# Hybrid decoder step (mLSTM and gated DeltaNet): residual rows loaded by halves, two weight pieces in gate buffers, one ring of three buffers for head outputs

## The chip, the cores and the metric

The kernel runs on one core of a Trainium2 chip. Its time is device microseconds from launch to end. Before the change the median of three runs is 1212.48 us (1211.23 to 1213.59). A traced execution gives the profile; times in it count from the span's first instruction.

## The reference

One layer of a decoder, for a prompt of 1024 tokens (with 16 learned tokens in front) and for 8 sample tokens with stored states:

```python
u = _rms_norm(x, norm_w) @ w_in              # 1024 -> 8216 columns
# split into q, k, v, o, z and gates of 4 mLSTM heads, q, k, v, z and gates of 8 GDN heads
hm = chunked mLSTM(q_m, k_m, v_m, li, lf)    # matrix memory, per head 128 x 256
ym = head_rms(hm) * w_mnorm * sigmoid(o_m) * silu(z_m)
og = chunked gated delta rule(silu(conv(q_g, k_g, v_g)), beta, g)   # state per head 128 x 128
yg = head_rms(og) * w_gnorm * silu(z_g)
y  = concat([ym, yg]) @ w_out                # 2048 -> 1024
return x + y, states                         # and a final RMSNorm with final_norm_w
```

All of it is float32. The outputs are both groups' rows and all new states.

## The kernel before

Every matrix product on TensorE (PE) takes its operands split into a high and a low part in a faster float32 format and adds three of the four partial products. The projection keeps the normalised, transposed x in SBUF (tiles xht and xlt, high and low part) and runs over 64 weight tiles of 128 columns. Between its matmuls PE gets the work of the heads: the chunk chains (`gdn_chain`, L1029, then `mlstm_chain`, L1264), their inverses, the sample group, and the gates (`gate`, L1473), which load a head's outputs from DRAM (tile ht), scale them on ScalarE (ACT), transpose them on PE (hT) and multiply them by the gate values.

The order of all instructions is written out by a planner at build time (`Plan`, L65). Each piece of work is a generator that yields what it waits for. `Plan.run` (L224) keeps a modelled clock for each engine and each time takes the first thread that can go on; the projection, followed by the output products, is the filler that runs otherwise. `note` (L99) advances the clocks; `Plan.old` holds, for tiles that come from a `Ring` (L245), the modelled end of the last read of the buffer, before which a write does not start. Tiles made by `w` (L453), two buffers deep unless stated, have no such entry. Each engine executes its instructions in the written order, and nearly all DMAs are issued in order on SyncE (SP).

Head outputs go through such tiles. A GDN chunk writes `oo` (L1094, 128 columns, two buffers) on VectorE (DVE), squares it on ACT and stores it to h_d in DRAM. An mLSTM chunk copies its numerator and denominator from PSUM to `mho` (L1335, 258 columns, two buffers) on ACT and stores it in the same way. Each head has a chunk 0 without an output and eight chunks with one.

The output projection is a Strassen-like scheme of seven products over two halves of the tokens and two halves of the columns (`PRODUCTS`, L1618; `out_products`, L1737). A product has eight steps k of four token tiles t, each three matmuls of 512 columns, 96 in all. Its right operands are four items made from pieces of W_out (512 KB each, 16 pieces): GpSimd (POOL) adds or subtracts two pieces (`right_sums`, L1678), ACT rounds the sum to the high part and DVE takes the low part (`right_splits`, L1699; tiles owh and owl). Its left operands are gate results, reloaded from DRAM (s_d, c_d; 256 KB each, `left_loads`, L1715) for every product after the first, and split by ACT and DVE. `drain` (L1770) adds or subtracts a finished product to rows of x, half a row of 512 columns at a time, on DVE: product 0 into the second halves (h = 1) of both token halves, product 1 into a second half, product 2 into first halves (h = 0). A product takes the PSUM banks of the one two before it, so those must be drained first.

`weight_loads` (L1654) loads the pieces in a fixed order into places that `places` (L1634) hands out: two buffers of the sample work (ebuf), two of the projection's weights (wout0, wout1), and, once the projection has ended (event "x") and xht and xlt are free, twelve of the 16 places there. Region places 12 and 13 hold sums, 14 the first residual rows, 15 the sample rows. Pieces 0 to 7 serve product 0, where item i is made from pieces 2i and 2i + 1. `residual` (L1812) loads eight tiles xr of 128 rows by 1024 columns (512 KB each) as the steps k = 4 to 7 of product 0 are used: one into the region, two into buffers of the ring r_v, five into the ring r_gm, which gates use for ht, y and yg and whose last five wait until gate 7 is through.

The profile puts all instructions on line L56, that of the helper that records them, so its rows are told apart by tile names.

Of the kernel before, what the change touches and what calls it, by code (L numbers as in the profile page):

```python
# [20 lines left out]
P = 128  # L21
D = 1024
# [42 lines left out]
class Plan:  # L65
# [102 lines left out]
    def shares(self, op, out, ins):  # L168
# [2 lines left out]
            return False  # L171
        return sum(int(np.prod(x.shape[1:])) > 1 for x in ins) > 1 or op in ("tensor_copy", "tensor_scalar", "memset")

    def when(self, x, wait):
        t, e = self.done.get(self.key(x), (0.0, ""))
        return t + (self.DMA if e == "dma" else wait + self.POOL * (e == "pool"))
# [68 lines left out]
class Ring:  # L245
# [7 lines left out]

    def get(self, *args):
        i = self.idle.pop(0)
        t, read = self.make(i, *args), self.plan.read
        self.old, self.names[i] = self.names.get(i), t.tensor.name
        read[t.tensor.name] = self.plan.old[t.tensor.name] = read.get(self.old, 0.0) + self.plan.LAT
        return i, t

    def free(self, i):
# [31 lines left out]
def hymba_kernel(ctx: ExitStack, tc: tile.TileContext, a: dict, o: dict):  # L293
# [157 lines left out]
    hs = gp.tile([P, 16, NS], F32, name="hs")  # L451

    def w(tag, shape, name, bufs=2):  # L453
        return wk.tile([P] + shape, F32, tag=tag, name=name, bufs=bufs)

    def ring(tag, bufs):
        tags = [f"{tag}{i}" for i in range(bufs)] + ["B", "E"]
# [6 lines left out]
    def has(*key):  # L464
        return lambda: key in done
# [563 lines left out]
    def gdn_chain(h):  # L1029
# [32 lines left out]
        for c in range(NCH):  # L1062
# [26 lines left out]
            if c == 0:  # L1089
                dve.tensor_copy(Sn, up[:, 0:P])  # L1090
            else:
                dve.scalar_tensor_tensor(
                    out=Sn, in0=S, scalar=egend[:, c, h : h + 1], in1=up[:, 0:P], op0=ALU.mult, op1=ALU.add)
                oo = w("oo", [P], f"oo{h}_{c}")  # L1094
                dve.tensor_tensor(out=oo, in0=qs, in1=up[:, P : 2 * P], op=ALU.add)
                jq = w("jm", [256], f"jo{h}_{c}", bufs=1)[:, 0:P]
                act.activation(jq, oo, AF.Square, accum_out=ss[:, 1, c - 1 : c])
                sp.dma_start(h_d[8 + h, :, c - 1, :], oo)
# [165 lines left out]
    def mlstm_chain(h):  # L1264
# [50 lines left out]
        for c in range(NCH):  # L1315
# [16 lines left out]
            if c + 1 < NCH:  # L1332
                prepare(c + 1)
            if c > 0:
                ho = w("mho", [258], f"mho{h}_{c}")  # L1335
                act.copy(ho[:, 0:257], nm[:, 0:257])
                st = w("st", [4], f"mst{h}_{c}")
                jk = w("jm", [256], f"mjk{h}_{c}", bufs=1)
# [295 lines left out]
    def places():  # L1634
# [4 lines left out]
        for i in range(2):  # L1639
            yield has("split", i)  # L1640
            t = wp.tile([P, 2 * HALF], F32, tag="wr", name=f"wout{i}")
            plan.read[t.tensor.name] = plan.read.get(wrs[-2], 0.0)
            wrs.append(t.tensor.name)
            yield t
        yield has("x")
        for tag, old in (("xh", xht), ("xl", xlt)):
            t = xp.tile([P, 32 * 264], F32, tag=tag, name=f"region{tag}")
# [1 line left out]
            plan.war.add(t.tensor.name)  # L1649
            region.extend(t[:, D * i : D * i + D] for i in range(8))  # L1650
        done.add(("region",))
        yield from region[0:12]

    def weight_loads():  # L1654

# [114 lines left out]
    def drain(p, t, pt):  # L1770

        to = PRODUCTS[p][1]
        yield lambda: all((c, t) in xr for c, _, _ in to) and (p == 0 or ("drain", p - 1, t) in done)
        for c, h, op in to:
            x_ = xr[c, t][:, HALF * h : HALF * h + HALF]
            yield x_
# [35 lines left out]
    def residual():  # L1812

        yield has("region")
        for n, (c, t) in enumerate([(c, t) for t in range(4) for c in range(2)]):
            if c == 0:
                yield has("used", 0, 4 + t)
            if n == 0:
                x_ = region[14]
            else:  # L1820
                r = r_v if n < 3 else r_gm
                yield lambda: len(pairs) == DEEP and r.can() and (n < 3 or ("y", 7) in done)
                _, x_ = r.get([D], f"xr{c}_{t}")
            q0 = HALF * c + P * t
            sp.dma_start(x_, a["x_p"][q0 : q0 + P, :])
            xr[c, t] = x_
        xs_ = region[15][0:NS]
        sp.dma_start(xs_, a["x_s"])
        xr["s"] = xs_
        yield has("product", 3)  # L1830
        sp.dma_start(fwb, a["final_w"].partition_broadcast(P))
        done.add(("fw",))
# [204 lines left out]
```

## Time and profile before

| | |
|---|---|
| median of three runs | 1212.48 us |
| the profiled execution | 1213.45 us, its span 1211.7 us |
| PE busy | 1190.0 us (98%) |
| DVE busy | 851.3 us (70%) |
| ACT busy | 602.7 us (50%) |
| POOL busy | 487.4 us (40%) |
| DMA | 154.86 MB, mean 128 GB/s |
| mean granted TensorE clock | 0.995 of full |
| chain that ended last | PE 84%, DVE 5%, issue 4%, DMA 3%, ACT 2% |

A matmul's end is modelled, so a busy PE is not a PE at its peak. SPq is SP's queue of DMA issues: a long duration of a merged row of issues means that the later of them waited. PEclk is the granted clock as a share of 2.4 GHz, and a DMA share of 1 means that all 16 engines are busy.

### The profile page before, as it was taken

What the parts mean: (1) busy time and instruction counts of PE and PEld (TensorE: products, weight loads), DVE (VectorE), ACT (ScalarE), POOL (GpSimd) and SP (SyncE); (2) the same over time, 40 slices, a digit from 0 to 9 for tenths busy, and PEclk for the clock granted to TensorE, in tenths of its full rate; (3) what the DMA queues carried; (4) which work ended last, traced back from release to release, by engine and by line L of the source; (5) the groups of instructions that cost most, each with busy time, mean ns of one, the idle gap of its engine ahead of it and who ended that gap; (6) DMA issues with size and microseconds to landing.
All of it is one profiled execution on the core that took longest, in us unless ns stands there. A gap on an engine that the chain in (4) does not pass through costs nothing.

```text
span 1211.7 us, 23025 instructions
## 1 busy us (share of the span) xinstructions
PE 1190.0 (98%) x8314; PEld 1109.5 (92%) x8314; DVE 851.3 (70%) x2069; ACT 602.7 (50%) x1894; POOL 487.4 (40%) x648
## 2 busy tenths in 40 slices
PE   9999999999999999999999999998999999989997
PEld 7999999999999999999998899988999999866885
DVE  6789787587968688863266565636666764779886
ACT  7544355667465656554545344434544433333544
POOL 3105877828584847773021413410011111442332
PEclk9999999999999999999999999998999999999999
DMA  6032213221211221122132343445777876682342
GB/s 240 19 98 86 77 47 88 80 61 55 84 58 43 85 78 51 45 65 58 46 102 79 142 142 109 143 148 161 264 275 285 301 287 225 248 309 86 98 157 87
DMA packets 85932, 154.86 MB, mean 128 GB/s; under 512 B 26665, under 2 KB 48385, under 8 KB 85818
## 3 DMA queue, kind: packets, MB, share of 16 engines
q1 hardware_dynamic: 85624, 153.23, 37.6%
q8 instruction: 65, 1.06, 0.4%
q14 instruction: 49, 0.40, 0.1%
q10 hardware_dynamic: 194, 0.17, 0.0%
HBM read 107.65 MB, written 45.71 MB: 127 GB/s over the span
## 4 chain that ended last, share of the span: by engine, by line
PE 84%; DVE 5%; issue 4%; DMA 3%; ACT 2%; POOL 1%; SPq 0%; POOLq 0%; ACTq 0%; DVEq 0%
PE pjg L56 20%; PE pjm L56 13%; PE op L56 11%; PE pjz L56 7%; PE pjo L56 7%; PE pjzm L56 6%; PE up L56 4%; PE tp L56 3%; PE sk L56 2%; PE mnm L56 2%; PE hT L56 1%; PE mup L56 1%; PE kk L56 1%; PE E L56 1%; PE W L56 1%
## 5 line engine op out<-in xcount | busy, mean ns | idle before, releaser
L56 PE MATMUL pjg<-xht,whg 128*128 128x350 f32 (+6 forms) x624 | 197.7, 324 | 1.0 <-ACT xht L56 1.0
L56 PE MATMUL pjg<-xlt,whg 128*128 128x350 f32 (+6 forms) x624 | 197.1, 323 | 0.0
L56 PE MATMUL pjg<-xht,wlg 128*128 128x350 f32 (+6 forms) x592 | 191.1, 326 | 0.0
L56 POOL TENSOR_TENSOR tmp<-B,E 33x31 f32<-33x31 f32 (+15 forms) x248 | 148.5, 599 | 76.0 <-DMA B<-nd 57.2
L56 POOL TENSOR_TENSOR E<-E,tmp 33x31 f32<-33x31 f32 (+15 forms) x248 | 155.2, 626 | 19.4
L56 PE MATMUL op<-owh,left 128*128 128x512 f32 x448 | 143.1, 399 | 1.8 <-DVE left L56 1.7
L56 PE MATMUL pjm<-xht,wlm 128*128 128x350 f32 (+2 forms) x384 | 126.4, 329 | 0.0
L56 PE MATMUL pjm<-xht,whm 128*128 128x350 f32 (+2 forms) x384 | 126.4, 329 | 0.0
L56 PE MATMUL pjm<-xlt,whm 128*128 128x350 f32 (+2 forms) x384 | 126.1, 328 | 0.0
L56 PEld LDWEIGHTS pjg<-xht,whg 128*128 128x128 f32 x624 | 116.5, 189 | 1.8 <-issue 1.2
L56 PEld LDWEIGHTS pjg<-xlt,whg 128*128 128x128 f32 x624 | 116.5, 189 | 0.5
L56 PEld LDWEIGHTS pjg<-xht,wlg 128*128 128x128 f32 x592 | 110.9, 189 | 0.4
L56 PEld LDWEIGHTS op<-owh,left 128*128 128x128 f32 x448 | 84.6, 189 | 24.8 <-DVE left L56 3.2
L56 DVE SCALAR_TENSOR_TENSOR kq<-cr,prm,kq 128x346 f32<-128x346 f32 (+7 forms) x147 | 92.7, 634 | 11.4 <-ACT kq L56 7.8
L56 PE MATMUL op<-owl,left 128*128 128x512 f32 x224 | 89.0, 397 | 2.1 <-DVE owl L56 2.1
L56 PEld LDWEIGHTS pjm<-xht,wlm 128*128 128x128 f32 x384 | 72.5, 189 | 0.8 <-issue 0.4
L56 PEld LDWEIGHTS pjm<-xlt,whm 128*128 128x128 f32 x384 | 72.4, 188 | 0.6 <-issue 0.4
L56 PEld LDWEIGHTS pjm<-xht,whm 128*128 128x128 f32 x384 | 72.4, 188 | 0.2
L56 POOL TENSOR_TENSOR ebuf<-ebuf,wb 128x1024 f32<-128x1024 f32 x8 | 15.4, 1930 | 129.4 <-DMA ebuf<-mvb_d 129.4
L56 PE MATMUL pjzm<-xlt,whzm 128*128 128x344 f32 x192 | 62.8, 327 | 0.0
L56 PE MATMUL pjz<-xlt,whz 128*128 128x344 f32 x192 | 62.8, 327 | 0.0
L56 PE MATMUL pjzm<-xht,wlzm 128*128 128x344 f32 x192 | 62.5, 326 | 0.0
(353 smaller groups left out, 3185.1 us busy)
## 6 DMA issues: line engine op xcount, KB each, us to landing
wrg<-in_wt SPq DMA_DIRECT2D x23, 512.0 KB
left<-c_d SPq DMA_DIRECT2D x40, 256.0 KB
wrm<-in_wt SPq DMA_DIRECT2D x16, 512.0 KB
ht<-h_d SPq DMA_DIRECT2D x16, 512.0 KB
gm<-rows_d SPq DMA_DIRECT2D x8, 576.0 KB
xt<-in_x_p SPq DMA_DIRECT2D x8, 512.0 KB
wrz<-in_wt SPq DMA_DIRECT2D x8, 512.0 KB
h_d<-oo SPq DMA_DIRECT2D x64, 64.0 KB
```

The lines of the kernel that those rows point to most:

```text
L56: r = f(*args, **kw)
```

## The change

The three edits, and one that goes with the third:

- The eight tiles xr are filled by halves. The second halves (256 KB each) are loaded as steps k = 0 to 3 of product 1 are used, the first halves as the same steps of product 2 are used. A drain waits for its own halves. Three tiles lie in the region (places 10, 11 and 14), two in r_v, three in r_gm.
- Weight pieces 4 and 5 go to two buffers of r_gm, once gate 5 and all GDN gates are through and two buffers are free; they no longer wait for the end of the projection. The region holds ten pieces.
- `oo` and `mho` become one tag of three buffers of 258 columns.
- `w` reports every tile that it makes to the planner, which then knows the last read of its buffer, as it did for rings.

```diff
--- before.py
+++ after.py
@@ -171,6 +171,10 @@
             return False
         return sum(int(np.prod(x.shape[1:])) > 1 for x in ins) > 1 or op in ("tensor_copy", "tensor_scalar", "memset")

+    def follow(self, t, old):
+
+        self.read[t.tensor.name] = self.old[t.tensor.name] = self.read.get(old, 0.0) + self.LAT
+
     def when(self, x, wait):
         t, e = self.done.get(self.key(x), (0.0, ""))
         return t + (self.DMA if e == "dma" else wait + self.POOL * (e == "pool"))
@@ -253,9 +257,9 @@

     def get(self, *args):
         i = self.idle.pop(0)
-        t, read = self.make(i, *args), self.plan.read
+        t = self.make(i, *args)
         self.old, self.names[i] = self.names.get(i), t.tensor.name
-        read[t.tensor.name] = self.plan.old[t.tensor.name] = read.get(self.old, 0.0) + self.plan.LAT
+        self.plan.follow(t, self.old)
         return i, t

     def free(self, i):
@@ -451,7 +455,12 @@
     hs = gp.tile([P, 16, NS], F32, name="hs")

     def w(tag, shape, name, bufs=2):
-        return wk.tile([P] + shape, F32, tag=tag, name=name, bufs=bufs)
+        t, names = wk.tile([P] + shape, F32, tag=tag, name=name, bufs=bufs), wnames.setdefault(tag, [""] * bufs)
+        plan.follow(t, names[-bufs])
+        names.append(t.tensor.name)
+        return t
+
+    wnames = {}

     def ring(tag, bufs):
         tags = [f"{tag}{i}" for i in range(bufs)] + ["B", "E"]
@@ -1091,7 +1100,7 @@
             else:
                 dve.scalar_tensor_tensor(
                     out=Sn, in0=S, scalar=egend[:, c, h : h + 1], in1=up[:, 0:P], op0=ALU.mult, op1=ALU.add)
-                oo = w("oo", [P], f"oo{h}_{c}")
+                oo = w("oo", [258], f"oo{h}_{c}", 3)[:, 0:P]
                 dve.tensor_tensor(out=oo, in0=qs, in1=up[:, P : 2 * P], op=ALU.add)
                 jq = w("jm", [256], f"jo{h}_{c}", bufs=1)[:, 0:P]
                 act.activation(jq, oo, AF.Square, accum_out=ss[:, 1, c - 1 : c])
@@ -1332,7 +1341,7 @@
             if c + 1 < NCH:
                 prepare(c + 1)
             if c > 0:
-                ho = w("mho", [258], f"mho{h}_{c}")
+                ho = w("oo", [258], f"mho{h}_{c}", 3)
                 act.copy(ho[:, 0:257], nm[:, 0:257])
                 st = w("st", [4], f"mst{h}_{c}")
                 jk = w("jm", [256], f"mjk{h}_{c}", bufs=1)
@@ -1642,6 +1651,11 @@
             plan.read[t.tensor.name] = plan.read.get(wrs[-2], 0.0)
             wrs.append(t.tensor.name)
             yield t
+        yield lambda: all(("y", k) in done for k in (5, *range(8, 16))) and r_gm.can(2)
+        for i in range(2):
+            t = r_gm.get([D], f"wout{2 + i}")[1]
+            yield plan.read[t.tensor.name]
+            yield t
         yield has("x")
         for tag, old in (("xh", xht), ("xl", xlt)):
             t = xp.tile([P, 32 * 264], F32, tag=tag, name=f"region{tag}")
@@ -1649,7 +1663,7 @@
             plan.war.add(t.tensor.name)
             region.extend(t[:, D * i : D * i + D] for i in range(8))
         done.add(("region",))
-        yield from region[0:12]
+        yield from region[0:10]

     def weight_loads():

@@ -1770,7 +1784,7 @@
     def drain(p, t, pt):

         to = PRODUCTS[p][1]
-        yield lambda: all((c, t) in xr for c, _, _ in to) and (p == 0 or ("drain", p - 1, t) in done)
+        yield lambda: all(("xr", c, h, t) in done for c, h, _ in to) and (p == 0 or ("drain", p - 1, t) in done)
         for c, h, op in to:
             x_ = xr[c, t][:, HALF * h : HALF * h + HALF]
             yield x_
@@ -1812,18 +1826,23 @@
     def residual():

         yield has("region")
-        for n, (c, t) in enumerate([(c, t) for t in range(4) for c in range(2)]):
-            if c == 0:
-                yield has("used", 0, 4 + t)
-            if n == 0:
-                x_ = region[14]
-            else:
-                r = r_v if n < 3 else r_gm
-                yield lambda: len(pairs) == DEEP and r.can() and (n < 3 or ("y", 7) in done)
-                _, x_ = r.get([D], f"xr{c}_{t}")
-            q0 = HALF * c + P * t
-            sp.dma_start(x_, a["x_p"][q0 : q0 + P, :])
-            xr[c, t] = x_
+        for h in (1, 0):
+            for t in range(4):
+                yield has("used", 2 - h, t)
+                for c in range(2):
+                    if h:
+                        n = 2 * t + c
+                        if n < 3:
+                            x_ = region[(10, 11, 14)[n]]
+                        else:
+                            r = r_v if n < 5 else r_gm
+                            yield lambda: len(pairs) == DEEP and r.can() and (n < 5 or ("y", 7) in done)
+                            x_ = r.get([D], f"xr{c}_{t}")[1]
+                            plan.split(x_, HALF, r.old)
+                        xr[c, t] = x_
+                    q0, hs_ = HALF * c + P * t, slice(HALF * h, HALF * h + HALF)
+                    sp.dma_start(xr[c, t][:, hs_], a["x_p"][q0 : q0 + P, hs_])
+                    done.add(("xr", c, h, t))
         xs_ = region[15][0:NS]
         sp.dma_start(xs_, a["x_s"])
         xr["s"] = xs_
```

## Rows read from the trace of the kernel before

**Rows 1.** Stretches of 30 us: length, busy time of each engine (instructions), PEclk, DMA share, GB/s.

```profile
0.00:30.00 30.00, 26.99 (x171) 23.22 (x172) 19.27 (x37) 21.01 (x44) 10.71 (x26) 1.00 0.65 242
...
810.00:840.00 30.00, 26.23 (x171) 23.96 (x161) 15.33 (x58) 15.60 (x55) 1.90 (x1) 1.00 0.51 162
...
840.00:870.00 30.00, 29.51 (x177) 28.67 (x178) 24.56 (x72) 17.10 (x54) 0.00 (x0) 0.89 0.63 209
...
1050.00:1080.00 30.00, 29.11 (x124) 22.75 (x122) 23.85 (x32) 8.09 (x15) 9.50 (x5) 1.00 0.84 321
...
1080.00:1110.00 30.00, 26.98 (x141) 16.99 (x141) 29.76 (x33) 11.88 (x23) 11.81 (x5) 0.94 0.25 81
```

**Rows 2.** Timeline of PE: start, us, instruction, then idle before and its releaser.

```profile
840.49 2.52 PE L56 MATMUL hT<-ident,ht 128*128 128x128 f32 x8 [3.09 <-ACT ht L56]
...
1074.85 0.73 PE L56 MATMUL op<-owh,left 128*128 128x512 f32 x2 [0.87 <-DVE left L56]
...
1082.20 0.64 PE L56 MATMUL op<-owl,left 128*128 128x512 f32 x1 [2.15 <-DVE owl L56]
```

**Rows 3.** Timeline of ACT, 831 to 843 us.

```profile
831.41 0.39 ACT L56 COPY mho<-mnm 128x257 f32<-128x257 f32 x1
...
839.23 0.38 ACT L56 COPY mho<-mnm 128x257 f32<-128x257 f32 x1 [6.54 <-DMA h_d<-mho]
...
840.05 2.43 ACT L56 ACTIVATE ht<-ht,rsg 128x128 f32<-128x128 f32 x8
```

**Rows 4.** Timeline of SP's DMA issues, 825 to 840 us.

```profile
825.50 0.36 SPq L56 DMA_DIRECT2D h_d<-mho  x1
...
826.92 1.67 SPq L56 DMA_DIRECT2D ht<-h_d  x1
...
828.69 0.29 SPq L56 DMA_DIRECT2D vb_d<-vsb  x1
...
832.27 0.32 SPq L56 DMA_DIRECT2D ebuf<-vb_d  x1
...
833.16 0.39 SPq L56 DMA_DIRECT2D h_d<-mho  x1
...
834.14 5.86 SPq L56 DMA_DIRECT2D h_d<-mho  x2
```

**Rows 5.** Stretches of 2 us, columns as in the first group.

```profile
842.00:844.00 2.00, 2.00 (x9) 1.78 (x9) 1.79 (x8) 1.64 (x5) 0.00 (x0) 0.50 0.00 0
...
1054.00:1056.00 2.00, 2.00 (x11) 1.59 (x10) 2.00 (x3) 0.47 (x1) 0.81 (x1) 1.00 0.01 5
...
1072.00:1074.00 2.00, 1.98 (x9) 1.27 (x7) 2.00 (x4) 0.81 (x2) 0.00 (x0) 1.00 1.02 366
```

**Rows 6.** The chain that ended last, out products: start, us, work.

```profile
1032.91 2.79 PE op L56 x12
...
1104.18 100.06 PE op L56 x429
```

**Rows 7.** Timeline of SP's DMA issues, 1050 to 1069 us.

```profile
1050.58 0.33 SPq L56 DMA_DIRECT2D left<-s_d  x1
...
1057.24 0.33 SPq L56 DMA_DIRECT2D xr<-in_x_p  x1
...
1059.92 1.39 SPq L56 DMA_DIRECT2D regionxh<-in_wo  x1
...
1068.46 0.33 SPq L56 DMA_DIRECT2D regionxl<-in_wo  x1
```

**Rows 8.** Timeline of POOL, 1068 to 1082 us.

```profile
1068.60 2.42 POOL L56 TENSOR_TENSOR regionxl<-regionxh 128x1024 f32<-128x1024 f32 x1 [13.79 <-DMA regionxh<-in_wo]
...
1076.44 5.15 POOL L56 TENSOR_TENSOR regionxl<-regionxl,regionxh 128x1024 f32<-128x1024 f32 x2 [5.43 <-DMA regionxl<-in_wo]
```

**Rows 9.** Timeline of ACT, around 1069 us.

```profile
1069.12 0.62 ACT L56 CAST left<-left 128x512 fp32r<-128x512 f32 x1 [11.80 <-DMA left<-s_d]
```

**Rows 10.** Instructions on the residual rows xr: durations min/median/max in ns.

```profile
L56 DVE TENSOR_TENSOR xr<-xr,op x42: 664/676/689, 1062.4 to 1204.3; 128x512 f32<-128x512 f32 x42
```

## The prediction

> **What bounds the kernel now.** TensorE. I read the page's busy times first: PE is busy 1190.0 of 1211.7 us, so 21.7 us is all the idle there is to win, beside a clock that is not always granted in full. The stretches of 30 us then say where that is [rows 1]: 3.0 us in the first stretch, 3.77 and 0.49 us at 810 to 870 us, 0.89 and 3.02 us at 1050 to 1110 us; behind the last matmul, at 1204.2 us (1104.18 + 100.06) [rows 6], the span has 7.5 us left. That makes 18.7 us; the other 3.0 us are spread over the rest of the kernel. The reader is also to see PEclk: it is 0.89 at 840 to 870 us and 0.94 at 1080 to 1110 us, in the two places right behind the longest gaps, and 1.00 in the others of the group [rows 1]. Inside the first it is 0.50, which is the 1.2 GHz level [rows 5]. A slice of 30 us at 0.89 loses about 0.11 x 30 = 3.3 us of TensorE's time, one at 0.94 about 1.8 us.
>
> PE's timeline names the gaps [rows 2]. At 837.4 us PE waits 3.09 us for the ACT scaling of a gate's rows ht. At 1074 us it waits 0.87 us for a left operand, and at 1080 us 2.15 us for the low half of a weight, both in the products of the output projection.
>
> **Three shared buffers for head outputs.** ACT began that ht scaling at 840.05 us with no idle of its own before it; what stood ahead of it in ACT's queue was the copy mho of chunk 8 of the last mLSTM head, which had waited 6.54 us for a DMA h_d<-mho [rows 3]. With two buffers chunk 8 overwrites chunk 6's. Chunk 6's store was issued only at 833.16 us, because SP stood between 828.69 and 832.27 us at a load that reads back what the issue before it wrote, and a weight load went in between [rows 4]. With three buffers chunk 8 waits for the store of chunk 5, issued at 825.50 us, before that blockage [rows 4]. From the store of chunk 5 at 825.50 us [rows 4] to the copy of chunk 7 at 831.41 us [rows 3] are two chunks, some 3 us each, so chunk 8's copy would start near 834.4 us and the scaling 0.8 us later (839.23 to 840.05 us [rows 3]), at 835.2 us. PE began 0.44 us after the scaling began (840.49 against 840.05 us [rows 2, 3]), so it would be free to go at 835.7 us, before it gets there at 837.4 us. The load of that ht was issued at 826.92 us [rows 4], 8 us before. What goes: 3.09 us of gap and 3.3 us of clock, 6.4 us. Next in line are the loads of the following gates: DMA share is 0.63 at 840 to 870 us [rows 1], and PE will ask 6.4 us sooner for what those loads bring. The bounds of what is given back are 0 and 6.4 us. I take 1, near the low end, since most of these loads are released by PE's own products and move with them. For the eight GDN heads the third buffer removes nothing that PE waited for.
>
> **Residual rows by halves, and later.** Before, eight loads of 512 KB are placed in SP's queue beside product 0. SP stands from 1050.9 to 1057.24 us at one of them, whose buffer gate 7 still reads, issues the last weight piece of product 1 at 1059.92 us and the first of product 2 at 1068.46 us [rows 7]. The DMAs run full then: share 1.02, 366 GB/s, so 512 KB cost 1.43 us [rows 5]. The pieces land so late that POOL stands 13.79 us for the first and 5.43 us for the second [rows 8], and ACT 11.80 us for the left operand queued among them [rows 9]. These are the origins of the two stalls.
>
> After, half the bytes (first halves, 2 MB) come in product 1 and the rest in product 2, where the DMA share is 0.25 [rows 1]. A product lasts 96 matmuls of 100.06/429 = 0.233 us, 22.4 us [rows 6]: product 1 starts at 1032.91 + 22.4 = 1055.3 us, product 2 is due at 1077.7 us. SP still stands until about 1057.3 us, for gate 7's two stores, next in its queue, wait for the same DVE work that releases that buffer at 1057.24 us [rows 7]. Behind them come the weight piece and two left operands of product 1: 2 MB with the stores, 5.7 us, so all have landed by about 1064 us. POOL's 2.42 us [rows 8] and four halves on ACT and DVE of 0.6 to 0.7 us each [rows 9, 10] later, 5.0 us in all, the weight is ready at 1069 us; PE wants it at three quarters of product 1, 1072.1 us. That stall goes (0.87 us). Then each of four steps brings a weight piece, a left operand and two half rows, 1.25 MB or 3.6 us. The first piece of product 2 lands near 1066 us instead of at 1076.44 us, so the second stall goes as well: 2.15 us and 1.8 us of clock. The fourth pair of half rows lands at 1064 + 4 x 3.6 = 1078.3 us, and two DVE additions of 0.68 us [rows 10] end at 1079.7 us; product 2 wants that PSUM bank at 1077.7 + 3 x 0.7 = 1079.8 us. This is the new latest arrival, and it has no slack. Its cost lies between 0 and the old stall with its clock, 4.0 us; I take 1. The eight additional issues cost SP some 0.4 us each, in stretches where it waits for PE anyway. The 0.87 us that is left of the idle at 1080 to 1110 us I let stand.
>
> For the smaller transfers I count bytes alone: the stretch at 1072 us carries 256 KB left operands among its loads and still moves 366 GB/s [rows 5]. The Trainium skill ("DMA: Bandwidth & Descriptors", Anatomy of one DMA and Bandwidth) speaks against halving: it gives each transfer 2.0 us beside its bytes over 436 GB/s, on the GpSimd path, and asks for at least 1 MiB. By that, with nothing overlapped, eight more loads would be an estimated 16 us more of queue and this edit a loss.
>
> **Two weight pieces in gate buffers.** Pieces 4 and 5 no longer wait for the end of the input projection: 1 MB, 2.9 us, leaves the busy start of product 0. PE did not wait there, so the gain is 0; it brings POOL's sums forward. The buffers are taken once gate 5 is through, leaving three for gates 6 and 7. If gate 7's second operand came late for it, its stores and with them the SP blockage would move; bounds 0 and 3 us, I take 0, because gate 6 gives its pair back before gate 7 asks.
>
> **The planner's new bounds.** No instruction is added, but every work tile's first write now has a bound from the last reader of its buffer, so the written-out order can change in the whole kernel. The 3.0 us of scattered idle may go or double; I take 0.5 us of loss.
>
> **The sum**, against the profiled execution (1213.45 us, span 1211.7): 1213.45 - 6.4 - 0.87 - 2.15 - 1.8 + 1 + 1 + 0.5 = 1204.7 us. That execution lies 0.97 us above the median of the runs, so I forecast 1204 us.
>
> **Rivals.**
> (a) Only the output products gain: the 837 us wait passes to the next gate's ht, for its load is late on a DMA that is busy up to 0.63. For it: the order of SP's queue is fixed, and the stores that blocked are still there. Against: PE has only 0.49 us of idle in the next 30 us [rows 1]. 1204.7 + 5.4 = 1210.1 less 1 for the median: 1209 us.
> (b) Only the head outputs gain: half rows or gate 7's stores hold product 2 up as before. For it: the 0.1 us of slack above; against: 1054 to 1056 us shows DMA share 0.01 [rows 5], capacity that earlier stores could use. 1204 + 3.8 = 1208 us.
> (c) The change doesn't do what it says: the new order puts other stalls where these were, each with its own half-speed tail; 1212 us.
> (d) Slower: the chains. Each head's chunk writes tiles two deep, and the planner now adds 0.2 us behind the last reader. If that bound holds back each of 64 GDN and 32 mLSTM chunk steps, the chain ends 96 x 0.2 = 19 us later, while the projection's jobs run out of buffers; once more than 11.2 us of it is seen by PE the whole gain is gone. All of it gives 1204 + 19 = 1223 us, a good half 1216 us. For it: the chain of heads ends at 840 us and gates wait for it [rows 2, 3]. Against: with some 3 us between chunks, a reader two chunks back is long done, and only stores read so late.
> (e) More than forecast: nothing given back, 1201 us.
>
> **How the numbers follow.** Forecast (1202 to 1206) 0.42, (a) 0.12, (b) 0.13, (c) 0.12, (d) 0.11, (e) 0.10. What a measurement of this kernel can tell is 0.2%, 2.4 us. Faster takes the forecast, (e), (b) and most of (a): 0.75; the same (c) and the rest: 0.14; slower (d): 0.11. The range for 8 in 10 is 1199 to 1212 us; within the likeliest case it is 1202 to 1206 us.
>
> **What would show it.** ACT's wait of mho for h_d gone, hT at 837 us without a gap, PEclk 1.00 at 840 to 870 us; POOL's wait before the last sum of product 1 down from 13.79 us to under 10; no PE gap over 1 us between 1070 and 1085 us. I am wrong if a gap over 2 us stands elsewhere behind 837 us, if DVE waits for xr at the start of product 2 for over 2 us, or if PE's scattered idle before 800 us grows by several us.

## The result and the profile after

The median went from 1212.93 us (4 runs) to 1203.76 us (4 runs, 1202.72 to 1206.82): a ratio of 0.9931, 95% interval 0.9909 to 0.9953. The forecast was 1204 us. The profiled execution took 1202.72 us, its span 1200.9 us, which is 10.8 us less than before; PE was busy 1184.0 us, so its idle time fell from 21.7 to 16.9 us, and the mean granted clock rose from 0.995 to 0.999. The time is right, but two steps of the sum were wrong in opposite directions, each by about 4 us or more, and made up for each other, as the experiments show.

The first view is the 30-us stretches of the kernel after, with the columns of [rows 1]:

```profile
810.00:840.00 30.00, 28.84 (x183) 27.05 (x182) 20.26 (x75) 18.64 (x64) 1.90 (x1) 1.00 0.52 171
840.00:870.00 30.00, 28.91 (x200) 27.83 (x199) 23.71 (x60) 14.97 (x45) 0.00 (x0) 1.00 0.75 265
870.00:900.00 30.00, 30.00 (x223) 28.71 (x222) 19.53 (x33) 14.47 (x43) 4.02 (x2) 1.00 0.76 273
1050.00:1080.00 30.00, 28.24 (x121) 22.27 (x120) 26.29 (x31) 10.75 (x20) 14.63 (x6) 1.00 0.74 268
1080.00:1110.00 30.00, 30.00 (x162) 19.88 (x162) 23.13 (x35) 10.23 (x20) 3.27 (x2) 1.00 0.45 140
```

The two slices that ran below the full clock before (0.89 and 0.94 in [rows 1]) are at 1.00. PE still waits 1.76 us in the stretch that holds the start of product 2. Its timeline (columns of [rows 2]) shows the waits of these stretches:

```profile
836.62 1.03 PE L56 MATMUL hT<-ident,ht 128*128 128x128 f32 x8
...
845.05 0.44 PE L56 MATMUL sosum<-wa,ones 128*128 128x64 f32 x2 [0.50 <-DVE wa L56]
846.08 0.43 PE L56 MATMUL pjo<-xht,who 128*128 128x344 f32 x1 [0.59 <-DVE mg L56]
...
1073.14 0.50 PE L56 MATMUL op<-owh,left 128*128 128x512 f32 x1 [0.33 <-DVE xr L56]
1075.53 0.50 PE L56 MATMUL op<-owh,left 128*128 128x512 f32 x1 [1.44 <-DVE xr L56]
```

The transposes hT that waited 3.09 us in [rows 2] now follow without a wait, and the eight of them take 1.03 us where they took 2.52. The two waits for left operand and weight in the products [rows 2] are gone, and so is the 0.87 us at 1080 to 1110 us that the prediction let stand; in their place PE waits for DVE's additions xr. ACT's timeline answers to [rows 3]:

```profile
833.06 0.37 ACT L56 COPY mho<-mnm 128x257 f32<-128x257 f32 x1 [0.99 <-PE mnm L56]
...
833.88 2.44 ACT L56 ACTIVATE ht<-ht,rsg 128x128 f32<-128x128 f32 x8
```

The copy no longer waits for a store; it waits for the matmul whose result it copies. The forecast for it was 834.4 us, and 835.2 us for the scaling. SP's queue of DMA issues answers to [rows 7]:

```profile
1046.90 0.32 SPq L56 DMA_DIRECT2D c_d<-ht  x1
1048.07 0.32 SPq L56 DMA_DIRECT2D c_d<-yg  x1
1048.44 0.46 SPq L56 DMA_DIRECT2D regionxh<-in_wo  x1
...
1061.46 1.01 SPq L56 DMA_DIRECT2D xr<-in_x_p  x2
```

and POOL's timeline of sums to [rows 8]:

```profile
1053.38 2.40 POOL L56 TENSOR_TENSOR regionxl<-regionxh 128x1024 f32<-128x1024 f32 x1 [8.30 <-DMA regionxh<-in_wo]
...
1060.26 2.59 POOL L56 TENSOR_TENSOR regionxl<-regionxh 128x1024 f32<-128x1024 f32 x1 [0.83 <-DMA regionxh<-in_wo]
1066.53 2.41 POOL L56 TENSOR_TENSOR regionxl<-regionxl,regionxh 128x1024 f32<-128x1024 f32 x1 [3.69 <-DVE owl L56]
1072.02 2.39 POOL L56 TENSOR_TENSOR regionxl<-regionxl,regionxh 128x1024 f32<-128x1024 f32 x1 [3.08 <-DVE owl L56]
```

Gate 7's stores (ht and yg) leave at 1046.90 us. In the kernel before, the first of them left behind the row load of 1057.24 us in [rows 7]:

```profile
1057.62 0.43 SPq L56 DMA_DIRECT2D c_d<-ht  x1
```

The prediction held that they would stay near 1057.3 us. Of the 10.7 us, 7.0 us are the earlier start of product 0 (1025.75 against 1032.75 us); counted from that start the stores leave after 21.2 us instead of 24.9 us. The weight piece for the last sum of product 1 is issued at 1048.44 instead of 1059.92 us, and POOL's longest wait in the products falls from 13.79 to 8.30 us.

### The profile page after: what moved, and what is told of

Read it like the earlier page. It is cut to its first block, busy times and chain, and to the rows that moved or that the text cites. A ratio compares the mean times of both kernels' runs of the same rounds, so it can differ in the third digit from the quotient of the medians.

```text
span 1200.9 us, 23024 instructions
## 1 busy us (share of the span) xinstructions
PE 1184.0 (99%) x8314; PEld 1105.9 (92%) x8314; DVE 852.2 (71%) x2069; ACT 602.4 (50%) x1894; POOL 487.9 (41%) x648
## 4 chain that ended last, share of the span: by engine, by line
PE 82%; DVE 9%; issue 5%; ACT 1%; POOL 1%; DMA 1%; POOLq 0%; SPq 0%; DVEq 0%; ACTq 0%
PE pjg L56 20%; PE pjm L56 13%; PE pjo L56 7%; PE pjz L56 7%; PE op L56 7%; PE pjzm L56 7%; PE up L56 4%; PE tp L56 3%; PE sk L56 2%; PE mnm L56 2%; DVE left L56 1%; PE mup L56 1%; PE hT L56 1%; DVE owl L56 1%; PE kk L56 1%
## 5 line engine op out<-in xcount | busy, mean ns | idle before, releaser
L56 PE MATMUL pjo<-xht,who 128*128 128x344 f32 x192 | 62.3, 324 | 0.6 <-DVE mg L56 0.6
L56 PE MATMUL pjz<-xht,wlz 128*128 128x344 f32 x192 | 62.4, 325 | 0.0
```

The lines of the kernel that those rows point to most:

```text
L56: r = f(*args, **kw)
```

## The experiments

Each was timed in five rounds against the kernel before; ratios are to that kernel on the same chip. On the chips of these runs the kernel before had medians of 1212.82 to 1214.18 us, so kernels of different rounds are compared by their ratios. One number from each profile splits the time well: the start of the first matmul of product 0 on PE's timeline, and what is left of the span from there. The left part carries the buffers and the planner, the right part the rows and the weights. Both columns come from one traced execution of each kernel.

| kernel | median us | ratio (95%) | product 0 starts | span behind it |
|---|---|---|---|---|
| before | 1212.93 | | 1032.75 | 179.0 |
| after | 1203.76 | 0.9931 (0.9909 to 0.9953) | 1025.75 | 175.2 |
| e1 buffers alone | 1209.48 | 0.9973 (0.9961 to 0.9985) | 1028.05 | 178.3 |
| e2 after, two buffers | 1212.68 | 0.9996 (0.9983 to 1.0008) | 1036.18 | 172.9 |
| e3 rows alone | 1213.08 | 0.9997 (0.9985 to 1.0009) | 1031.86 | 179.7 |
| e4 planner alone | 1217.47 | 1.0035 (1.0022 to 1.0048) | 1036.06 | 179.7 |
| e5 weights alone | 1205.33 | 0.9937 (0.9916 to 0.9958) | 1031.22 | 172.5 |
| e6 after, no weights | 1208.56 | 0.9960 (0.9945 to 0.9974) | 1027.73 | 179.2 |
| e7 after, old rows | 1201.37 | 0.9905 (0.9888 to 0.9923) | 1027.77 | 172.4 |
| e8 after, rows one step sooner | 1202.01 | 0.9916 (0.9898 to 0.9935) | 1026.52 | 172.9 |
| e9 after, again | 1203.80 | 0.9927 (0.9912 to 0.9943) | 1026.83 | 175.8 |
| e10 e7, pieces not early | 1203.96 | 0.9920 (0.9900 to 0.9939) | 1026.74 | 174.1 |
| e11 after, halves at the old time | 1202.63 | 0.9911 (0.9893 to 0.9929) | 1027.97 | 172.8 |
| e12 e7, a row in the way | 1206.85 | 0.9949 (0.9930 to 0.9967) | 1029.12 | 176.2 |

**e1_buffers_only**: the kernel before with the one ring of three buffers.

```diff
-                oo = w("oo", [P], f"oo{h}_{c}")
+                oo = w("oo", [258], f"oo{h}_{c}", 3)[:, 0:P]
...
-                ho = w("mho", [258], f"mho{h}_{c}")
+                ho = w("oo", [258], f"mho{h}_{c}", 3)
```

> The kernel before with one edit: head outputs of both kinds share one tag of three buffers. Theory (the copy of chunk 8 waits for a store that a third buffer takes out of its way, and that wait makes the 3.09 us gap at 837 us and its half-speed tail): about 6.4 us less than before, 1205.5 to 1207.5 us; the gap at 837 us gone, PEclk 1.00 behind it, the gaps in the output products (0.87 and 2.15 us) still there, each 6 to 7 us earlier. Rival (it is the planner's knowledge of the buffers that moves the waiting work): no change, 1211 us or more, with the gap in place. Rival (what is won at 837 us is given back to the loads of later gates): under 3 us of gain, with new PE gaps before the output products.

Measured: 0.27% less, about 3.3 us. The gap at 837 us is gone and products start 4.7 us earlier. But in this execution part is given back at a later gate. PE's timeline of e1:

```profile
869.84 0.32 PE L56 MATMUL pjzm<-xht,wlzm 128*128 128x344 f32 x1
...
871.16 2.45 PE L56 MATMUL hT<-ident,ht 128*128 128x128 f32 x8 [0.68 <-ACT ht L56]
...
874.27 0.49 PE L56 MATMUL pjzm<-xht,wlzm 128*128 128x344 f32 x1
```

and stretches of 2 us of e1 (columns of [rows 1]):

```profile
872.00:874.00 2.00, 2.00 (x9) 1.34 (x9) 1.10 (x2) 1.16 (x4) 0.00 (x0) 0.84 1.04 420
874.00:876.00 2.00, 2.00 (x9) 2.00 (x9) 1.08 (x3) 0.97 (x2) 1.20 (x1) 0.50 1.02 416
```

The wait shown is 0.68 us, and the eight transposes behind it take 2.45 us where those of the same gate take 1.30 us in the kernel after: ACT, which scales their slices, was itself kept 3.37 us by the load of ht and takes 2.45 us for the eight. PE counts as busy in that time. Then the granted clock falls to 0.50, the 1.2 GHz level, and a matmul of 0.32 us lasts 0.49. So rival (a) of the prediction is true in part, but not in every execution. The nine kernels with three buffers run the same instructions in the same order on every engine up to about 1010 us, as their traces show. At this gate PE waits between nothing and 1.01 us in them, and the clock of 870 to 900 us is below 1.00 in two (0.94, in e1 and e12). Transposes as slow stand at this gate in the kernel before, too (2.38 us behind a wait of 0.32 us), there without a loss of clock. The output products keep two of their three waits (2.16 us for owl, 0.89 us for left): nothing there was changed.

**e2_two_buffers**: the kernel after with e1's two lines turned back.

```diff
-                oo = w("oo", [258], f"oo{h}_{c}", 3)[:, 0:P]
+                oo = w("oo", [P], f"oo{h}_{c}")
...
-                ho = w("oo", [258], f"mho{h}_{c}", 3)
+                ho = w("mho", [258], f"mho{h}_{c}")
```

> The changed kernel with the two buffers of each kind put back (the planner still knows the readers of work tiles). Theory: the store still holds the copy of chunk 8, so some 6 us of the gain are lost again, 1208 to 1211 us, with ACT's wait for the store of head outputs back. Rival (the planner is what counts): it now sees the wait, writes other work ahead of it, and the time stays below 1206 us.

Measured: no gain left over the kernel before. Products start 3.4 us later than before, and the part behind is 6.1 us shorter. The late start isn't the old gap, but a new one on PE's timeline, at the sample group's sum:

```profile
850.11 0.44 PE L56 MATMUL sosum<-wa,ones 128*128 128x64 f32 x2 [3.67 <-DVE wa L56]
```

That comes from the planner's edit, which with two buffers writes another order; e4 has the same row alone.

**e4_planner_only**: the kernel before with the planner told of every work tile's buffer.

```diff
+    def follow(self, t, old):
+        self.read[t.tensor.name] = self.old[t.tensor.name] = self.read.get(old, 0.0) + self.LAT
...
-        return wk.tile([P] + shape, F32, tag=tag, name=name, bufs=bufs)
+        t, names = wk.tile([P] + shape, F32, tag=tag, name=name, bufs=bufs), wnames.setdefault(tag, [""] * bufs)
+        plan.follow(t, names[-bufs])
+        names.append(t.tensor.name)
+        return t
...
```

> The kernel before with one edit: the planner is told the last readers of work tiles. Theory: no wait and no transfer changes, within 1.5 us of before, 1211.5 to 1214.5 us. Rival (the planner writes other work ahead of the copy that waits): 1206 to 1210 us. Rival (the added bounds hold back the chains of the heads): 1216 us or more.

Measured: 0.35% slower, 4.2 us. PE's timeline shows the cost; the chain's gap of [rows 2] at 837 us is not in it, but a longer one ten us later (and 2.44 us of wait at 957 us):

```profile
850.92 0.43 PE L56 MATMUL sosum<-wa,ones 128*128 128x64 f32 x2 [3.66 <-DVE wa L56]
```

Up to 837 us every engine runs the order of before. There, with two buffers, the planner seems to see the late copy and to move work around it, and the order that it then writes waits at another place. With three buffers the bounds move nothing that the traces show: e8, e11 and e12, which have this edit, run the same order as e1, which lacks it, on every engine up to about 1010 us, where the early weight pieces begin. So within the change the edit shows no cost.

**e3_rows_only**: the kernel before with the residual rows loaded by halves and later, in the places of before.

```diff
-            if c == 0:
-                yield has("used", 0, 4 + t)
...
+        for h in (1, 0):
+            for t in range(4):
+                yield has("used", 2 - h, t)
...
+                    sp.dma_start(xr[c, t][:, hs_], a["x_p"][q0 : q0 + P, hs_])
```

> The kernel before with one edit: residual rows by halves and later, in the places they had (one in the region, two in the ring of values, five in gate buffers). Theory (the weight pieces came late because 4 MB of rows stood ahead of them): both stalls of the output products shrink, some 3.5 us less than before, 1208.5 to 1210.5 us, the gap at 837 us unchanged. Rival (the two early weight pieces bring the gain in the output products): within 1 us of before.

Measured: no difference. This is the step that the forecast gave 4.8 us. Both stalls that it was to remove are gone, and three others stand there on PE's timeline:

```profile
1079.54 0.50 PE L56 MATMUL op<-owh,left 128*128 128x512 f32 x1 [1.28 <-DVE xr L56]
1082.55 0.80 PE L56 MATMUL op<-owh,left 128*128 128x512 f32 x1 [2.03 <-DVE xr L56]
1084.94 0.80 PE L56 MATMUL op<-owh,left 128*128 128x512 f32 x1 [0.74 <-DVE xr L56]
```

Together 4.05 us, against 0.87 + 2.15 us [rows 2], and the clock of 1080 to 1110 us is 0.89 (before 0.94). Gate 7's stores leave at 1054.96 us, 2.7 us sooner than before.

**e5_weights_only**: the kernel before with weight pieces 4 and 5 in gate buffers; the rows move into the region places that become free, but are loaded whole and at the old time.

```diff
+        yield lambda: all(("y", k) in done for k in (5, *range(8, 16))) and r_gm.can(2)
+        for i in range(2):
+            t = r_gm.get([D], f"wout{2 + i}")[1]
+            yield plan.read[t.tensor.name]
+            yield t
...
-        yield from region[0:12]
+        yield from region[0:10]
...
-            if n == 0:
-                x_ = region[14]
+            if n < 3:
+                x_ = region[(10, 11, 14)[n]]
...
```

> The kernel before with one edit: weight pieces 4 and 5 in gate buffers before the projection ends, and for it three residual rows in the region; rows whole and at their old time, two buffers for head outputs. Theory (the early pieces make the gain in the output products by themselves): the gap at 837 us stays, no PE gap over 0.5 us after it, 1206 to 1209 us. Rival (early pieces only help together with the shared buffers): 1211 us or more.

Measured: 0.63% faster, 7.6 us; the part behind the start of product 0 falls from 179.0 to 172.5 us, and PE waits for nothing from 1031 to 1110 us. This is the step to which the forecast gave nothing. SP's queue shows how:

```profile
1049.96 0.38 SPq L56 DMA_DIRECT2D xr<-in_x_p  x1
1052.33 0.33 SPq L56 DMA_DIRECT2D c_d<-ht  x1
1053.53 0.33 SPq L56 DMA_DIRECT2D c_d<-yg  x1
1053.91 0.47 SPq L56 DMA_DIRECT2D regionxh<-in_wo  x1
```

No row load waits ahead of gate 7's stores: the first rows go to the region, and the others are queued behind the stores. SP's stand from 1050.9 to 1057.24 us [rows 7] is gone.

**e6_no_weights**: the kernel after without that edit.

```diff
-        yield lambda: all(("y", k) in done for k in (5, *range(8, 16))) and r_gm.can(2)
...
-        yield from region[0:10]
+        yield from region[0:12]
...
-                        if n < 3:
-                            x_ = region[(10, 11, 14)[n]]
+                        if n < 1:
+                            x_ = region[14]
...
```

> The changed kernel without the move of two weight pieces (residual rows in the places they had before, but by halves and later; shared buffers). Theory now (rows alone only turn the two stalls into waits of product 2 for DVE's additions, since DVE starts the splits of product 1 too late; the early weight pieces start them sooner): about the time of the shared buffers alone, 1208 to 1211 us, with three PE waits for the residual additions, some 4 us, behind product 1. Rival (the weight pieces bring nothing, as predicted): 1203 to 1205.5 us.

Measured: 1208.56 us. Products start 5.0 us sooner than before, but the part behind is 179.2 us, none of it gained: PE waits 0.28, 2.04 and 1.43 us for xr between 1074 and 1080 us. So with late half rows the products gain nothing without the weight edit.

**e7_old_rows**: the kernel after with whole rows at the old time, in the new places.

```diff
-        for h in (1, 0):
-            for t in range(4):
-                yield has("used", 2 - h, t)
...
+        for n, (c, t) in enumerate([(c, t) for t in range(4) for c in range(2)]):
+            if c == 0:
+                yield has("used", 0, 4 + t)
...
```

> The changed kernel with the residual rows loaded whole and at their old time (two weight pieces in gate buffers and shared buffers kept). Theory (rows and weight pieces only gain together, for the rows stand ahead of the weight pieces of products 1 and 2): 1207 to 1211 us, with the PE wait for a weight's low half behind product 1 near 2 us. Rival (the weight pieces alone make the gain in the output products): 1203 to 1205.5 us.

Measured: 1201.37 us (1200.86 to 1202.02), the fastest median of all, and below e9, the changed kernel, on the same chip; the intervals of the two ratios overlap a little (0.9888 to 0.9923 and 0.9912 to 0.9943), and the ranges of their single runs (e9 1202.63 to 1205.46) don't. The stretches of the products show nothing lost:

```profile
1050.00:1080.00 30.00, 30.00 (x130) 24.25 (x130) 25.67 (x35) 12.36 (x22) 12.45 (x5) 1.00 0.81 299
1080.00:1110.00 30.00, 30.00 (x162) 19.88 (x161) 25.77 (x37) 10.12 (x21) 5.97 (x3) 1.00 0.26 80
```

and in SP's queue gate 7's stores leave 21.1 us after the start of product 0:

```profile
1048.88 0.33 SPq L56 DMA_DIRECT2D c_d<-ht  x1
1050.09 0.33 SPq L56 DMA_DIRECT2D c_d<-yg  x1
```

**e8_rows_sooner** and **e9_again**: the kernel after with the second halves asked for one step sooner, and the kernel after once more beside it.

```diff
-                yield has("used", 2 - h, t)
+                yield has("used", 0, 6) if h and t == 0 else has("used", 2 - h, max(t - h, 0))
```

> The changed kernel with the second halves of the residual rows asked for one step sooner (the first pair at step 6 of product 0, the others one step of product 1 earlier). Theory (the 1.8 us that product 2 waits are DVE's queue, which idles 3.7 us in product 1 where the first two additions would fit): the PE waits for residual additions fall under 0.6 us and the time by 1 to 2 us against the changed kernel in the same job. Rival (the halves land too late, DMA bound): no change, or worse, since the halves then stand ahead of a weight piece.

> The changed kernel again, unaltered, for comparison in this job: 1202 to 1206 us; the waits of product 2 for residual additions 1.4 to 2 us as in its first profile.

Measured: 1202.01 against 1203.80 us. PE has no wait for xr in e8; in e9 it waits 0.98 and 1.43 us.

**e11_halves_not_late**: the kernel after, its second halves asked for at the old time, at steps 4 to 7 of product 0. It parts the halving from the lateness.

```diff
-                yield has("used", 2 - h, t)
+                yield has("used", 0, 4 + t) if h else has("used", 2, t)
```

> The changed kernel with the second halves of the rows asked for at steps 4 to 7 of product 0, as whole rows were before, and the first halves still in product 2. Theory (the halves cost nothing, their lateness makes product 2 wait for the residual additions): no PE wait for residual additions over 0.3 us behind product 1, 1200.5 to 1202.5 us. Rival (the halved transfers are what DVE waits for): the waits of 1.4 to 2.4 us stay, 1203 us or more.

Measured: 1202.63 us, 172.8 us behind the start of product 0 (e7 172.4), no wait for xr. Loading by halves costs nothing that this can show. Asking late goes with 2 to 3 us more in the part behind (175.2 and 175.8 us against 172.4 to 172.9) and with 1.2 to 2.4 us in the medians, where the intervals of the ratios overlap. The reason is on DVE's timeline of the kernel after:

```profile
1056.47 3.51 DVE L56 TENSOR_TENSOR owl<-regionxl,owh 128x512 fp32r<-128x512 f32 x2 [3.71 <-ACT owh L56]
1059.90 4.10 DVE L56 TENSOR_TENSOR left<-left 128x512 fp32r<-128x512 f32 x3
1063.92 1.27 DVE L56 TENSOR_TENSOR regionxl<-regionxl,op 128x512 f32<-128x512 f32 x2
...
1066.92 2.57 DVE L56 TENSOR_TENSOR left<-left 128x512 fp32r<-128x512 f32 x1
...
1073.61 2.47 DVE L56 TENSOR_TENSOR xr<-xr,op 128x512 f32<-128x512 f32 x4
```

Product 0's first additions come at 1063.92 us, behind splits that waited for a weight and then ran slowly, and the later ones are spread up to 1076 us in a queue that has no idle time from 1056.47 us on. Product 2 needs the PSUM banks that they free. The margin is some 2 us: e2 has the same late rows in the same order on DVE in this stretch and no wait for xr, and there the three splits of left operands take 1.88 us instead of 4.10. In the kernel after, POOL's sum of 1060.26 us runs into the second of them; in e2 the sum begins together with the third, and it is the sum that takes longer, 2.97 us:

```profile
1069.33 1.88 DVE L56 TENSOR_TENSOR left<-left 128x512 fp32r<-128x512 f32 x3
1071.13 1.27 DVE L56 TENSOR_TENSOR regionxl<-regionxl,op 128x512 f32<-128x512 f32 x2
...
1070.52 2.97 POOL L56 TENSOR_TENSOR regionxl<-regionxh 128x1024 f32<-128x1024 f32 x1 [1.66 <-DMA regionxh<-in_wo]
```

The additions of 1071.13 us come 35.0 us after product 0's start, against 38.2 us in the kernel after. In e11 the first additions come sooner, at 1052.83 us:

```profile
1052.83 1.28 DVE L56 TENSOR_TENSOR regionxl<-regionxl,op 128x512 f32<-128x512 f32 x2
```

**e10_pieces_late**: e7, with the gate buffers used for the last two pieces; pieces 4 and 5 again wait for the end of the projection. The rows' places stay.

```diff
-        yield lambda: all(("y", k) in done for k in (5, *range(8, 16))) and r_gm.can(2)
...
         yield from region[0:10]
+        yield lambda: all(("y", k) in done for k in (7, *range(8, 16))) and r_gm.can(2)
...
```

> The changed kernel with whole rows at their old time and with the gate buffers given to the last two weight pieces instead of pieces 4 and 5, which are loaded into the region after the projection as before; three rows stay in the region. Theory (what counts is that pieces 4 and 5 are early: POOL's sum of item 2 waits for them, DVE's splits wait for POOL, gate 7's sums stand behind these on DVE, and gate 7's stores hold SP): POOL waits some 10 us again for the sum of item 2, gate 7's first store is issued some 3 us later in product 0, and a PE gap of 1 us or more is back behind product 1; 1204.5 to 1208.5 us. Rival (what counts is that no row load waits for gate 7's buffer in SP's queue any more, by its place in the region): no gap, 1201 to 1203 us.

Measured: 1203.96 us, between the two theories' ranges. POOL stands for the third item's pieces again, and PE waits once in the products. POOL's timeline of e10:

```profile
1032.04 4.94 POOL L56 TENSOR_TENSOR regionxl<-regionxh 128x1024 f32<-128x1024 f32 x2 [11.55 <-DMA regionxh<-in_wo]
```

and PE's timeline:

```profile
1079.88 0.73 PE L56 MATMUL op<-owh,left 128*128 128x512 f32 x2 [1.40 <-DVE left L56]
```

**e12_row_in_the_way**: e7 with the rows in other places, so that the third and fourth row load stand in SP's queue ahead of gate 7's stores, in buffers that gates use. The pieces stay early.

```diff
-            if n < 3:
-                x_ = region[(10, 11, 14)[n]]
+            if n in (0, 6, 7):
+                x_ = region[{0: 14, 6: 10, 7: 11}[n]]
...
-                r = r_v if n < 5 else r_gm
-                yield lambda: len(pairs) == DEEP and r.can() and (n < 5 or ("y", 7) in done)
+                r = r_v if n < 3 else r_gm
+                yield lambda: len(pairs) == DEEP and r.can() and (n < 4 or ("y", 7) in done)
```

> The kernel of e7_old_rows (three buffers, weight pieces 4 and 5 early, whole rows at the old time) with the rows in other places: rows 4 to 6 take gate buffers and rows 7 and 8 the two places of the region, and row 4 stands in SP's queue ahead of gate 7's two stores, as before the change. It tells apart what the early pieces do by themselves from what the rows' places do. Theory, the early pieces are what counts for more: gate 7's DVE work is done early, as in e7, so the row waits little and the stores still leave before 1051 us; time 1201 to 1203 us, no TensorE gap over 1 us between 1070 and 1090 us. Rival, the row in the queue is what counts: SP stands at it until gate 7 is through, the stores leave past 1053 us, gaps of 1 to 3 us come back between 1070 and 1090 us; time 1204 to 1208 us.

Measured: 1206.85 us, in the rival's range; the theory fell. SP's queue:

```profile
1051.14 0.81 SPq L56 DMA_DIRECT2D xr<-in_x_p  x2
1052.00 0.42 SPq L56 DMA_DIRECT2D c_d<-ht  x1
...
1058.95 1.43 SPq L56 DMA_DIRECT2D xr<-in_x_p  x2
```

and what SP waited for from 1045 to 1075 us (us in total, times, longest):

```profile
SPq L56 <- DMA c_d<-ht: 4.6, 1, 4.6
...
SPq L56 <- DVE yg L56: 3.8, 1, 3.8
```

SP stands 3.8 us at a row whose buffer gate 7's yg work still reads, and 4.6 us at one whose buffer the store of ht reads. POOL then stands 12.06 us for the last sum of product 1, PE 1.34, 0.37 and 1.21 us in the products. e1, e10, e12 and e7 are the four cases of two questions, all with three buffers: pieces early or not, rows out of the way or not. Rows out of the way take 0.9973 to 0.9920 without early pieces and 0.9949 to 0.9905 with them; in neither pair do the intervals meet. Early pieces take 0.9973 to 0.9949 and 0.9920 to 0.9905; in both pairs they overlap. So the places of the rows are shown to count, by 5 to 6 us; the earliness of the pieces is likely worth 2 to 3 us. Two things blur the sizes: e12 has a second stand of SP, the 4.6 us behind the stores, where the kernel before waits 0.8 us for that store, and e10 loads the last two pieces into gate buffers, which e1 does not. How much is due to the one load ahead of the stores is therefore not shown.

## Why the prediction was right in the sum and wrong in a step

**Three shared buffers: right, near the size.** All three signs came: the wait of ACT's copy gone, hT at 837 us without a gap, PEclk 1.00 at 840 to 870 us. The forecast was 5.4 us net. Over the nine kernels with three buffers product 0 starts at 1025.75 to 1029.12 us, mean 1027.4; over the three with two buffers and the planner of before (before, e3, e5) at 1031.22 to 1032.75, mean 1031.9: 4.6 us. The sum missed a term of its own row: hT of 2.52 us in [rows 2] lasts 1.03 us when ACT is done ahead, so up to 1.5 us more went; part of it may already be in the 3.3 us of clock. And more than 1 us came back: 1.09 us in the kernel after (0.50 + 0.59), a late hT with its clock in e1. By medians the edit is worth 3 to 4.5 us (e1 alone; e5 to e7, 0.9937 to 0.9905; e3 to e6, 0.9997 to 0.9960).

**Rows by halves and later: wrong. This is the step that failed.** It held that the weight pieces came late because of the rows' bytes ahead of them, and that moving the rows behind would take away 4.8 us for 1 us of new lateness. Alone it gave nothing (e3), and on top of the other edits the late asking cost 2 to 3 us by the profiles, 1.2 to 2.4 us by the medians (e8, e11 and e7 against after and e9). The first stalls did go, but the bytes weren't what made them: in e5 and e7 the same 4 MB come whole and at the old time, and both stalls are gone as well. What e3, e5 and e7 have in common is that no row load that waits for a gate's buffer stands ahead of gate 7's stores. What replaced the stalls was named, the additions at the start of product 2, but not its cause: the forecast counted bytes to a last pair at 1078.3 us. The last half rows of product 0 were issued by 1062.5 us, and what held the additions up was DVE's queue.

**Two weight pieces: wrong; forecast 0, measured about 6.5 us.** The step looked at PE, which did not wait in product 0, and at the pieces themselves. It did not follow the other half of the edit: two region places fall free, rows go there, and the load that SP stood at for 6.3 us [rows 7] is no longer ahead of the stores. The prediction even wrote that gate 7's stores wait for the same DVE work as that row, so SP would stand until 1057.3 us anyhow. But the store of ht needs earlier work than the row, whose buffer was free only after yg: in e7 it leaves 1.2 us ahead of the store of yg, and 21.1 us after product 0's start instead of 24.9 us. How the 6.5 us divide between the rows' places and the early pieces is told at e12. That the products gained 3.8 us in the profile (179.0 to 175.2), as much as the sum had for both steps (0.87 + 2.15 + 1.8 - 1), is chance: 6.5 us won (e5) less 2.7 us lost with the late rows.

**The planner's bounds: forecast 0.5 us of loss, none seen.** With three buffers no order changes up to the products (e8, e11 and e12 against e1). Alone it is the slower case (e4), but not by rival (d)'s mechanism: no chain is held back step by step, for the order up to 837 us is that of before; behind it PE waits 3.66 and 2.44 us at two places.

Of the signs set out ahead, one failed: a PE gap over 1 us stands between 1070 and 1085 us (1.44 us).

**Halves and their number.** In the kernel after, DMA moves 391 to 405 GB/s from 1062 to 1068 us, with loads of 256 KB in the queue:

```profile
1062.00:1064.00 2.00, 2.00 (x10) 1.67 (x9) 2.00 (x3) 0.00 (x0) 0.84 (x1) 1.00 1.07 405
1064.00:1066.00 2.00, 2.00 (x10) 1.62 (x9) 2.00 (x4) 1.30 (x3) 0.00 (x0) 1.00 1.01 391
```

Eight more loads cost nothing clear of the noise (e11), so counting bytes alone served here. The Trainium skill ("DMA: Bandwidth & Descriptors", Anatomy of one DMA and Bandwidth) would have added an estimated 16 us of queue at 2.0 us each, if nothing overlapped; its 2.0 us are for the GpSimd path. The trace does not agree for SP's queue: the loads overlap there, at the rates above.

## What to carry to other kernels

When an edit frees a buffer, follow who moves into it and what that takes out of an in-order queue: row loads that wait for a buffer, ahead of two stores that don't, cost this kernel some 5 us. Loading later was worth nothing by itself; what it delays runs in some engine's queue, and that queue's idle time there, not the DMA's, says whether there is room. Telling a planner the truth can make its order worse while the wait that it now sees is still there; take the wait away first.

## What the runs showed of the hardware

**Busy is not at work, and a short wait can cost clock or not.** Eight transposes that follow ACT slice by slice count as 2.45 us of busy PE, and the granted clock fell to 0.50 right after them although the idle time shown is 0.68 us (e1). The same gate's transposes in e5 left it at 1.00, in all of 870 to 900 us:

```profile
875.90 2.37 PE L56 MATMUL hT<-ident,ht 128*128 128x128 f32 x8 [0.55 <-ACT ht L56]
```

So they did in e3 behind a longer wait of 0.93 us (2.38 us for the eight). After a wait of 1.44 us at 1074.09 us (kernel after), with ordinary matmuls before and behind, the clock stayed at 1.00; after one of 2.15 us in the kernel before it is 0.94 [rows 1, 2]. What decides between these cases is not shown.

**DVE loses the time of a POOL sum.** A DVE split of 0.68 us lasts 2.57 us at 1066.92 us, while POOL's sum runs from 1066.53 to 1068.94 us, and ends 0.55 us after it. The additions at 1073.61 us, one operand of which is in PSUM, take 0.67 us each, as without POOL, although a POOL sum runs until 1074.41 us. The Trainium skill ("SBUF — State Buffer", SBUF: two separate sides) says why: a DVE operation with two inputs in SBUF and a GpSimd operation that reads SBUF exclude each other for the whole instruction, and the one that starts first goes through. The trace agrees in both rows, and in e2, where the sum of 1070.52 us is the one that takes longer. In the kernel after, three POOL sums between 1056 and 1069 us cost DVE 1.9 to 2.2 us each; those that found DVE idle (1053.38 us) or at additions from PSUM (1072.02 us) cost it nothing. That is how a queue that is 71% busy over the span had no room there.
